# Which queue loads three of the five input tiles of a two-layer attention/FFN step

## The chip, the cores and the metric

The kernel runs on one NeuronCore of a Trainium2 chip. Five engines work side by side and meet at semaphores: TensorE (PE in the profile, its weight loads PEld), VectorE (DVE), ScalarE (ACT), GpSimd (POOL) and SyncE (SP). SyncE computes nothing; it issues transfers. ScalarE can issue transfers too, from its own queue, in between its computing instructions and in their order. The metric is the device time of one execution in microseconds (us); the median of several runs counts.

## The reference, cut to what matters

The program is one inference step of a trunk with two layers, over 512 latent tokens (`x_sample`) and 128 context tokens (`x_prompt`), all float32. What bears on this change is the very beginning of layer 0: all five tiles of 128 tokens are RMS-normalised, scaled and shifted by a modulation (adaLN), and multiplied by the q, k, v weights.

```
def rmsnorm(x, g):
    xf = x.astype(jnp.float32)
    y = xf * lax.rsqrt(jnp.mean(xf * xf, axis=-1, keepdims=True) + EPS)
    return (y * g.astype(jnp.float32)).astype(x.dtype)

def adaln(cond, w, b):
    m = jax.nn.silu(cond) @ w + b
    return jnp.split(m[..., None, :], 6, axis=-1)
...
    for l in range(DEPTH):
        sh_ap, sc_ap, g_ap, sh_fp, sc_fp, g_fp = adaln(c_ctx, ada_w[l], ada_b[l])
        sh_as, sc_as, g_as, sh_fs, sc_fs, g_fs = adaln(c, ada_w[l], ada_b[l])
        hp = rmsnorm(xp, norm_mix_pre[l]) * (1.0 + sc_ap) + sh_ap
        hs = rmsnorm(xs, norm_mix_pre[l]) * (1.0 + sc_as) + sh_as
        if l % N_MIXERS == 0:
            qp, kp, vp = na_qkv(hp, na_w_qkv[i])
            op = blocked_attention(qp, kp, vp)
            qs, ks_, vs = na_qkv(hs, na_w_qkv[i])
            os_ = neighbourhood_attention(qs, ks_, vs, cache_na_k[:, i], cache_na_v[:, i], na_rpb[i])
...
```

## The kernel before

The tokens are five tiles of 128: latent tiles 0 to 3 and the prompt as tile 4, each 128 partitions by 1024 floats (512 KB). They are loaded once into `x0_0` to `x0_4` (the profile calls all of them `x`). The latent tokens form a grid of 8 rows by 64 columns, and latent tile t takes 16 of its columns: the access pattern has 16 steps of one token (4 KB) outside and 8 steps of 64 tokens (256 KB) inside. The prompt tile is one contiguous block.

The opening (lines 505 to 668) runs so:

- `x_load(t)` issues the load of tile t on SyncE. `const_loads` follows the first one and issues four small pieces into `cc` (conditioning vectors, biases, gains) and the 128x128 identity `ident`.
- A product of `cc` and `ident` turns the conditioning into columns `ct`; ScalarE applies SiLU and writes `scol` (L525).
- `x_norm(t)`: ScalarE squares and sums the tile (`junk`, `ss`, L539), GpSimd makes `rstd` of it (L204, L206), VectorE multiplies the tile (L541).
- `x_turn(t)`: TensorE transposes the tile in two halves of four 128x128 blocks into `tr` banks of PSUM; ScalarE copies the first half to `xT` (L553) and VectorE the second (L551). Five of eight banks are held by the value projection, so the halves go round through three banks, and a half can start only when the copy three halves earlier is done.
- `mod_rows(i)` and `mod_cols(i)`, i from 0 to 3: the modulation weights `wf` (four loads of 512 KB each, from `ada_w`) against `scolp` into `row` (PE); ScalarE copies `row` to `rs` (L574); PE turns that into columns `col`; VectorE makes the gains `gcol` and shifts `hcol` (L589 to L591); then ScalarE writes `hT[0]` (L596) and VectorE updates `xT` (L597) and writes the low part `hT[1]` (L598).
- `wsplit` loads q, k, v weights into `wr`; ScalarE casts them into `wh` (L178) and VectorE or GpSimd subtracts into `wl` (L180). `v_part` multiplies `hT` by them into `vp`.
- `na_v_cache` loads a cached value tile `vc` from ScalarE's queue (L491) and copies it to `vt` (L487).

The order in which each engine takes these instructions is set by the tile framework's scheduler when the program is built; the order of PE is fixed by hand (each PE instruction is chained to the one before). Transfers of SyncE and ScalarE share eight semaphores (`DMAHW0` to `DMAHW7`) in turn, and a transfer is issued only when the one that had its semaphore before has landed.

Of the kernel before, what the change touches and what calls it, by code (L numbers as in the profile page):

```python
# [20 lines left out]
D = 1024  # L21
# [4 lines left out]
NT = T // P  # L26
# [5 lines left out]
GW = 64  # L32
# [40 lines left out]
def raw_ap(ap, offset, dims):  # L73
    return bass.AP(tensor=ap.tensor, offset=ap.offset + offset, ap=[list(d) for d in dims])
# [30 lines left out]
def hybrid_step(ctx: ExitStack, tc: tile.TileContext, A, O):  # L105
    nc = tc.nc
# [58 lines left out]
    def x_in(t):  # L165
        return A["x_sample"][0, t * P : (t + 1) * P, :] if t < 4 else A["x_prompt"][0]
# [35 lines left out]
    def rstd_of(ss, n):  # L202
        v = sm.tile([P, 1], F32, name="var")
        nc.gpsimd.tensor_scalar(v, ss, 1.0 / n, EPS, op0=ALU.mult, op1=ALU.add)  # L204
        r = sm.tile([P, 1], F32, name="rstd")
        nc.gpsimd.tensor_tensor(r, v, mhalf, op=ALU.pow)  # L206
        return r
# [298 lines left out]
    with ExitStack() as s:  # L506
        sp = s.enter_context(pool("st"))
        xts = []

        def x_load(t):  # L510
            xt = sp.tile([P, D], F32, name=f"x0_{t}")
            if t < 4:
                nc.sync.dma_start(xt, raw_ap(A["x_sample"], 16 * t * D, [[D, 16], [GW * D, 8], [1, D]]))
            else:
                nc.sync.dma_start(xt, x_in(t))
            xts.append(xt)

        x_load(0)
        const_loads()
        sel = sp.tile([P, 2], F32, name="sel")  # L520
# [14 lines left out]
        def x_norm(t):  # L535
            xt = xts[t]
            ss = sm.tile([P, 1], F32, name="ss")
            junk = sp.tile([P, D], BF16, tag="junk", name="junk0")
            nc.scalar.activation(junk, xt, AF.Square, accum_out=ss)  # L539
            r = rstd_of(ss, D)  # L540
            nc.vector.tensor_scalar(xt, xt, r, None, op0=ALU.mult)  # L541
# [14 lines left out]
        def mod_load(i):  # L556
            out = {}
            for n in range(2):
                for h in range(2):
                    out[n, h] = sp.tile([P, 4, 256], F32, tag="wf", name="wf", bufs=7)  # L560
                    nc.sync.dma_start(out[n, h], rows(A["ada_w"][0], 4 * h, 4, D - D * n + 256 * i, 256))
            return out
# [41 lines left out]
        def wv_load(i):  # L604
            wv[i] = wsplit(rows(wqkv, 4 * i, 4, 2048, 256), 4, 256)

        def x_in_norm(ts):
            for t in ts:
                if t:
                    x_load(t)  # L610
                x_norm(t)

        x_in_norm(range(NT))
        loads[0] = mod_load(0)
        wv_load(0)
        loads[1] = mod_load(1)
# [1345 lines left out]
```

## Time and profile before

| | |
|---|---|
| time, median of 3 runs | 1548.16 us (1547.85 to 1550.32) |
| profiled execution | 1550.43 us, span of its instructions 1548.6 us |
| PE busy | 1513.5 us (98%) |
| DVE, ACT, POOL busy | 1022.3 (66%), 854.0 (55%), 702.2 (45%) us |
| DMA | 243.99 MB, mean 158 GB/s |

The span is cut in the profile into stretches and instructions, each with its start in us from the span's start. "Idle before" is the time for which an engine stood before the instruction, and the name behind the arrow is what ended it.

### The profile page before, as it was taken

The numbers are of one execution on the slowest core, as the hardware profiler recorded it, in microseconds if no ns is written. First come the engines' busy times: TensorE is split into PE (matmuls) and PEld (weight loads), VectorE is DVE, ScalarE is ACT, GpSimd is POOL, SyncE is SP. The second block draws the span as 40 slices with busy tenths as digits, with TensorE's granted clock in tenths as the row PEclk, the third lists the DMA queues.
The fourth block names the chain that finished last, engine by engine and source line by source line (L and its number), as shares of the span: only waits on it lengthen the run. The fifth ranks groups of instructions, "written<-read, shape, count | busy, mean of one in ns | idle before, by whom it ended". The sixth has DMA issues, their size and how long they took to land.

```text
span 1548.6 us, 26098 instructions
## 1 busy us (share of the span) xinstructions
PE 1513.5 (98%) x9709; PEld 1343.4 (87%) x9709; DVE 1022.3 (66%) x1648; ACT 854.0 (55%) x1624; POOL 702.2 (45%) x606
## 2 busy tenths in 40 slices
PE   6999999999999999999999999999999999999998
PEld 5988998888999999978887878778899999988886
DVE  4553343659877666755757877773988887786554
ACT  5664564646655555554544447763665665564443
POOL 1554564432355455525443464532235666542433
PEclk9999999999999999999999999999999999999999
DMA  9745454253565665388574421015433335447664
GB/s 324 199 123 161 121 134 116 64 189 125 176 225 182 222 190 162 111 279 272 174 238 153 131 67 44 2 34 196 153 115 114 120 110 158 132 161 251 226 220 131
DMA packets 196666, 243.99 MB, mean 158 GB/s; under 512 B 11484, under 2 KB 153020, under 8 KB 196540
## 3 DMA queue, kind: packets, MB, share of 16 engines
q1 hardware_dynamic: 186704, 235.74, 47.8%
q10 hardware_dynamic: 9836, 6.59, 2.5%
q8 instruction: 76, 1.25, 0.3%
q14 instruction: 50, 0.41, 0.1%
HBM read 214.38 MB, written 26.34 MB: 155 GB/s over the span
## 4 chain that ended last, share of the span: by engine, by line
PE 63%; DVE 5%; ACT 2%; issue 2%; POOL 2%; DMA 1%; POOLq 0%; DVEq 0%; ACTq 0%
PE ux L117 18%; PE acc L117 17%; PE uz L117 8%; PE gp L117 5%; PE uy L117 4%; PE po L117 3%; PE y L117 2%; PE s L117 2%; PE tp L120 2%; PE ada L117 1%; DMA wr<-in_ffn_w_down 1%; DVE t L1281 1%; POOL wl L180 1%; DMA wr<-in_ffn_w_up 1%; DVE wl L180 1%
## 5 line engine op out<-in xcount | busy, mean ns | idle before, releaser
L180 POOL TENSOR_TENSOR wl<-wr,wh 128x1024 fp32r<-128x1024 f32 x70 | 173.8, 2487 | 239.8 <-ACT wh L178 228.7
L1204 POOL TENSOR_TENSOR wl<-wr,wh 128x1024 fp32r<-128x1024 f32 x76 | 183.6, 2438 | 46.9 <-ACT wh L1203 43.3
L117 PE MATMUL ux<-B,wh 128*128 128x322 f32 x832 | 200.0, 311 | 0.9 <-ACT u L1258 0.9
L1281 DVE SCALAR_TENSOR_TENSOR t<-C,cw,t 128x644 f32<-128x644 f32 x176 | 156.4, 888 | 51.3 <-ACT t L1279 50.7
L178 ACT CAST wh<-wr 128x1024 fp32r<-128x1024 f32 x140 | 145.5, 1048 | 53.8 <-DMA wr<-in_ffn_w_down 41.1
L117 PE MATMUL acc<-wh,alo 128*128 128x512 f32 x440 | 172.3, 392 | 0.3 <-DVE alo L1173 0.3
L117 PE MATMUL acc<-wl,ahi 128*128 128x512 f32 x440 | 171.9, 391 | 0.5 <-POOL wl L180 0.5
L117 PE MATMUL acc<-wh,ahi 128*128 128x512 f32 x440 | 171.9, 391 | 0.0
L117 PE MATMUL uz<-B,wh 128*128 128x322 f32 x640 | 156.2, 312 | 0.9 <-ACT v L1258 0.9
L117 PEld LDWEIGHTS ux<-B,wh 128*128 128x128 f32 x832 | 143.6, 189 | 3.3 <-issue 1.2
L1173 DVE TENSOR_TENSOR alo<-ain,ahi 128x384 fp32r<-128x384 f32 (+1 forms) x88 | 81.8, 948 | 88.9 <-ACT ahi L1171 88.6
L117 PE MATMUL ux<-B,wl 128*128 128x322 f32 x416 | 129.5, 311 | 3.0 <-DVE wl L1204 3.0
L117 PE MATMUL qk<-hT,wh 128*128 128x384 f32 (+1 forms) x512 | 122.3, 315 | 0.0
L117 PEld LDWEIGHTS uz<-B,wh 128*128 128x128 f32 x640 | 110.9, 189 | 4.4 <-ACT v L1258 1.5
L1204 POOL TENSOR_TENSOR vl<-wr,vh 128x1024 fp32r<-128x1024 f32 x38 | 96.4, 2537 | 24.6 <-ACT vh L1203 24.3
L1203 ACT CAST wh<-wr 128x1024 fp32r<-128x1024 f32 x84 | 84.8, 1049 | 40.9 <-DVE wr L1227 40.6
L1279 ACT ACTIVATE t<-C,cw 128x644 f32<-128x644 f32 x88 | 78.6, 893 | 47.8 <-DVE C L1309 40.2
L180 DVE TENSOR_TENSOR wl<-wr,wh 128x1024 fp32r<-128x1024 f32 x70 | 91.4, 1315 | 19.3 <-ACT wh L178 18.7
L117 PE MATMUL uz<-B,wl 128*128 128x322 f32 x320 | 99.6, 311 | 0.3 <-POOL wl L1204 0.3
L117 PEld LDWEIGHTS acc<-wl,ahi 128*128 128x128 f32 x440 | 82.6, 188 | 18.9 <-POOL wl L180 0.9
L117 PEld LDWEIGHTS acc<-wh,alo 128*128 128x128 f32 x440 | 82.5, 188 | 18.7 <-DVE alo L1173 1.1
L117 PEld LDWEIGHTS acc<-wh,ahi 128*128 128x128 f32 x440 | 82.6, 188 | 17.7
(259 smaller groups left out, 3858.2 us busy)
## 6 DMA issues: line engine op xcount, KB each, us to landing
wr<-in_ffn_w_up SPq DMA_DIRECT2D x88, 512.0 KB
wr<-in_ffn_w_down SPq DMA_DIRECT2D x88, 512.0 KB
wr<-in_ada_w SPq DMA_DIRECT2D x72, 512.0 KB
act<-act SPq DMA_DIRECT2D x44, 321.0 KB
wr<-in_na_w_qkv SPq DMA_DIRECT2D x24, 512.0 KB
mod<-modrow SPq DMA_DIRECT2D x20, 512.0 KB
ain<-act SPq DMA_DIRECT2D x44, 192.0 KB
wf<-in_ada_w SPq DMA_DIRECT2D x16, 512.0 KB
```

The source lines that it names most:

```text
L117: pe(nc.tensor.matmul(*a, **k))
L120: pe(nc.tensor.transpose(*a, **k))
L178: i = nc.scalar.copy(hi, raw)
L180: j = (low or nc.vector).tensor_sub(lo, raw, f32(hi))
L1173: pin(nc.vector.tensor_sub(lo[:, 0 : c1 - c0], ain[:, 0 : c1 - c0], f32(hi[:, 0 : c1 - c0])))
L1203: nc.scalar.copy(hl[0], src)
L1204: low.tensor_sub(hl[1], src, f32(hl[0]))
L1279: nc.scalar.activation(t, taps(0), AF.Identity, bias=cw[:, 3, n : n + 1], scale=cw[:, 1, n : n + 1])
L1281: nc.vector.scalar_tensor_tensor(t, taps(d), cw[:, w, n : n + 1], t, op0=ALU.mult, op1=ALU.add)
```

## The change

Latent tiles 2 and 3 and the prompt tile are issued on ScalarE's queue; tiles 0 and 1 stay with SyncE. The four later loads are written out in the order 2, 3, 4, 1 before any of the norms, where each load stood ahead of its own norm before. The list `xts` is put back in the order of the tiles, so that norms and turns go on in the order 0 to 4.

```
@@ x_load
             if t < 4:
-                nc.sync.dma_start(xt, raw_ap(A["x_sample"], 16 * t * D, [[D, 16], [GW * D, 8], [1, D]]))
+                q = nc.scalar if t >= 2 else nc.sync
+                q.dma_start(xt, raw_ap(A["x_sample"], 16 * t * D, [[D, 16], [GW * D, 8], [1, D]]))
             else:
-                nc.sync.dma_start(xt, x_in(t))
+                nc.scalar.dma_start(xt, x_in(t))
@@ the loop over tiles
-        def x_in_norm(ts):
-            for t in ts:
-                if t:
-                    x_load(t)
-                x_norm(t)
-
-        x_in_norm(range(NT))
+        for t in (2, 3, 4, 1):
+            x_load(t)
+        xts[1:] = xts[4], *xts[1:4]
+        for t in range(NT):
+            x_norm(t)
```

The scheduler orders the opening anew on SP, ACT and DVE. PE's order is the same, and so is everything behind the opening. Names such as `x_2_155` are tile 2 of the input with a buffer number.

On SyncE, from the first transfer on, this stands before:

```order
L513 DMA x_0_134<-in_x_sample 128x1x1024
L146 DMA cc<-in_c 8x128
L147 DMA cc<-in_c_ctx 8x128
L148 DMA cc<-in_ada_b 16x128
L149 DMA cc<-in_norm_mix_pre 8x128
L150 DMA ident<-in_k_ident 128x128
L513 DMA x_1_163<-in_x_sample 128x1x1024
L513 DMA x_2_173<-in_x_sample 128x1x1024 [waits DMAHW0_49]
L513 DMA x_3_183<-in_x_sample 128x1x1024 [waits DMAHW1_49]
L515 DMA x_4_193<-in_x_prompt 128x1024 [waits DMAHW2_49]
L561 DMA wf<-in_ada_w 128x4x256 [waits DMAHW3_49]
```

and this in the change, with the semaphores waited for:

```order
L514 DMA x_0_134<-in_x_sample 128x1x1024
L146 DMA cc<-in_c 8x128
L147 DMA cc<-in_c_ctx 8x128
L148 DMA cc<-in_ada_b 16x128
L149 DMA cc<-in_norm_mix_pre 8x128
L150 DMA ident<-in_k_ident 128x128
L514 DMA x_1_161<-in_x_sample 128x1x1024 [waits DMAHW0_49]
L562 DMA wf<-in_ada_w 128x4x256 [waits DMAHW2_49]
```

Three transfers are gone from SyncE, and tile 1 now waits for a semaphore before it is issued.

On ScalarE, from its first instruction to the square of tile 4, this stands before:

```order
L491 DMA vc<-in_cache_na_v 128x256
L158 ACT_TABLE_LOAD
L158 ACTIVATE cw_78<-mhalf 128x1 [waits Pool_49]
L487 COPY vt<-vc 128x256 [waits DMAHW0_49]
L539 ACTIVATE junk_156,ss<-x_0_134 128x1024 [waits DMAHW1_49]
L525 ACTIVATE scol<-ct 128x16 [waits PE_49]
L539 ACTIVATE junk_166,ss<-x_1_163 128x1024 [waits DMAHW7_49,Activation_49]
L539 ACTIVATE junk_176,ss<-x_2_173 128x1024 [waits DMAHW0_49,Activation_49]
L553 COPY xT<-tr 128x4x128 [waits PE_49] x2
L539 ACTIVATE junk_186,ss<-x_3_183 128x1024 [waits DMAHW1_49,Activation_49]
L553 COPY xT<-tr 128x4x128 [waits PE_49]
L539 ACTIVATE junk_196,ss<-x_4_193 128x1024 [waits DMAHW2_49,Activation_49,Pool_49]
```

and this in the change, from its fourth instruction on:

```order
L514 DMA x_3_157<-in_x_sample 128x1x1024
L516 DMA x_4_159<-in_x_prompt 128x1024 [waits DMAHW1_49]
L526 ACTIVATE scol<-ct 128x16 [waits PE_49]
L540 ACTIVATE junk_164,ss<-x_0_134 128x1024
L491 DMA vc<-in_cache_na_v 128x256 [waits DMAHW4_49]
L540 ACTIVATE junk_172,ss<-x_1_161 128x1024 [waits DMAHW0_49,Activation_49]
L540 ACTIVATE junk_180,ss<-x_2_155 128x1024 [waits Activation_49]
L487 COPY vt<-vc 128x256 [waits DMAHW4_49]
L540 ACTIVATE junk_188,ss<-x_3_157 128x1024 [waits DMAHW5_49,Activation_49]
L554 COPY xT<-tr 128x4x128 [waits PE_49]
L540 ACTIVATE junk_196,ss<-x_4_159 128x1024 [waits DMAHW1_49,Activation_49,Pool_49]
L554 COPY xT<-tr 128x4x128 [waits PE_49] x3
```

`scol` stands ahead of the square of tile 0 now, the load and copy of `vc` stand among the squares, and the first copy to `xT` comes behind the square of tile 3, where it came behind that of tile 2. (The first instruction of ScalarE is now the load of tile 2.) Tile 1 waits for `DMAHW0`, the semaphore of tile 2, which went first: the square of tile 2 needs no wait for its own transfer behind that of tile 1. Tile 4 waits for `DMAHW1`, that of tile 0: the square of tile 0 has no wait for a transfer any more.

On VectorE, from the multiplication of tile 3 to the first low part of `hT`, this stands before:

```order
L541 TENSOR_SCALAR x_3_183<-x_3_183,rstd 128x1024
L541 TENSOR_SCALAR x_4_193<-x_4_193,rstd 128x1024
L551 COPY xT<-tr 128x4x128 x2
L589 SCALAR_TENSOR_TENSOR gcol<-col,colb 128x4
L591 TENSOR_TENSOR hcol<-col,colb 128x4
L590 TENSOR_TENSOR gcol<-gcol,colb 128x4
L180 TENSOR_TENSOR wl<-wr,wh 128x1024
L597 TENSOR_SCALAR xT<-xT,gcol,hcol 128x512
L597 TENSOR_SCALAR xT<-xT,gcol,hcol 128x128
L597 TENSOR_SCALAR xT<-xT,gcol,hcol 128x512
L598 TENSOR_TENSOR hT_123<-xT,hT_122 128x640
```

and this in the change:

```order
L542 TENSOR_SCALAR x_4_159<-x_4_159,rstd 128x1024
L552 COPY xT<-tr 128x4x128 x3
L180 TENSOR_TENSOR wl<-wr,wh 128x1024
L590 SCALAR_TENSOR_TENSOR gcol<-col,colb 128x4
L592 TENSOR_TENSOR hcol<-col,colb 128x4
L591 TENSOR_TENSOR gcol<-gcol,colb 128x4
L598 TENSOR_SCALAR xT<-xT,gcol,hcol 128x512
L598 TENSOR_SCALAR xT<-xT,gcol,hcol 128x128
L599 TENSOR_TENSOR hT_123<-xT,hT_122 128x640
```

The subtraction into `wl` has moved from behind `gcol` to ahead of it, and the low part of `hT` comes behind two instructions on `xT`, where it came behind three. ScalarE's cast into `wh`, from which `wl` is made, has moved up in the same way, ahead of the last copy to `xT`.

## Rows read from the trace of the kernel before

**Rows 1.** The page: span, and busy time of the engines

```profile
span 1548.6 us, 26098 instructions
PE 1513.5 (98%) x9709; PEld 1343.4 (87%) x9709; DVE 1022.3 (66%) x1648; ACT 854.0 (55%) x1624; POOL 702.2 (45%) x606
```

**Rows 2.** Stretches: busy by engine (instructions), granted clock, DMA share, GB/s

```profile
19.00:22.30 3.30, 3.30 (x30) 1.86 (x32) 0.69 (x1) 0.59 (x1) 0.00 (x0) 0.52 1.09 372
...
26.70:36.00 9.30, 7.93 (x84) 6.66 (x81) 6.23 (x15) 4.63 (x9) 0.00 (x0) 1.00 1.09 383
36.00:60.00 24.00, 24.00 (x210) 22.75 (x209) 11.20 (x24) 13.27 (x23) 11.05 (x14) 1.00 0.90 228
```

**Rows 3.** Timeline of SyncE: start, duration, transfers issued

```profile
0.72 0.68 SPq L513 DMA_DIRECT2D x<-in_x_sample  x1
...
3.06 0.36 SPq L150 DMA_DIRECT2D ident<-in_k_ident  x1
3.46 2.85 SPq L513 DMA_DIRECT2D x<-in_x_sample  x3
...
7.00 4.35 SPq L561 DMA_DIRECT2D wf<-in_ada_w  x4
```

**Rows 4.** Timeline of ScalarE, the opening

```profile
0.72 0.40 ACTq L491 DMA_DIRECT2D vc<-in_cache_na_v  x1
...
3.02 0.40 ACT L487 COPY vt<-vc 128x256 f32<-128x256 f32 x1 [0.36 <-DMA vc<-in_cache_na_v]
5.78 1.06 ACT L539 ACTIVATE junk<-x 128x1024 bf16<-128x1024 f32 x1 [2.36 <-DMA x<-in_x_sample]
...
7.40 0.18 ACT L525 ACTIVATE scol<-ct 128x16 f32<-128x16 f32 x1 [0.47 <-PE ct L120]
8.36 1.06 ACT L539 ACTIVATE junk<-x 128x1024 bf16<-128x1024 f32 x1 [0.78 <-DMA x<-in_x_sample]
...
10.53 1.06 ACT L539 ACTIVATE junk<-x 128x1024 bf16<-128x1024 f32 x1 [1.01 <-DMA x<-in_x_sample]
...
11.58 0.57 ACT L553 COPY xT<-tr 128x512 f32<-128x512 f32 x1
...
15.13 1.06 ACT L539 ACTIVATE junk<-x 128x1024 bf16<-128x1024 f32 x1
```

**Rows 5.** Transfers from 7 to 12.5 us, latent tiles alone moving

```profile
DMA packets 369, 1.32 MB, mean 241 GB/s; under 512 B 46, under 2 KB 46, under 8 KB 369
```

**Rows 6.** Transfers from 13.5 to 38 us, weights

```profile
DMA packets 9457, 9.36 MB, mean 382 GB/s; under 512 B 285, under 2 KB 9456, under 8 KB 9456
```

**Rows 7.** Timeline of PE, the opening

```profile
8.70 1.97 PE L120 MATMUL tr<-ident,x 128*128 128x128 f32 x8 [1.34 <-DVE x L541]
...
17.00 1.06 PE L120 MATMUL tr<-ident,x 128*128 128x128 f32 x8 [1.54 <-DVE x L541]
18.47 1.69 PE L120 MATMUL tr<-ident,x 128*128 128x128 f32 x8 [0.41 <-DVE x L541]
20.09 2.93 PE L117 MATMUL row<-wf,scolp 128*32 128x256 f32 x32
...
24.72 2.03 PE L117 MATMUL row<-wf,scolp 128*32 128x256 f32 x32
...
28.55 0.50 PE L117 MATMUL vp<-wh,hT 128*128 128x256 f32 x2 [1.37 <-DVE hT L598]
```

**Rows 8.** Timeline of VectorE, the opening

```profile
6.96 0.17 DVE L521 TENSOR_REDUCE sel<-ident 128x2 f32<-128x8 f32 x1 [6.96 <-DMA ident<-in_k_ident]
...
17.57 0.75 DVE L541 TENSOR_SCALAR x<-x,rstd 128x1024 f32<-128x1024 f32 x1 [0.72 <-POOL rstd L206]
...
25.02 0.16 DVE L590 TENSOR_TENSOR gcol<-gcol,colb 128x4 f32<-128x4 f32 x1
25.10 1.22 DVE L180 TENSOR_TENSOR wl<-wr,wh 128x1024 fp32r<-128x1024 f32 x1
...
27.68 0.82 DVE L598 TENSOR_TENSOR hT<-xT,hT 128x640 fp32r<-128x640 f32 x1
```

## The prediction

> **What bounds the kernel now.** I read the page first: PE is busy for 1513.5 of 1548.6 us [rows 1], so the kernel is bound by TensorE, and a change outside of it can only count where TensorE stands. Next I cut the first 60 us, where the change lies, into stretches. From 36 us on PE is busy for the whole 24.00 us, and from 26.7 to 36 it stands for 9.30 - 7.93 = 1.37 us [rows 2]. The reader should take two things from that: whatever makes PE reach its value products earlier or later passes on to the end one for one, since nothing behind takes up slack; and the only slack close by is that 1.37 us, which the timeline of PE shows as one stand before 28.55, ended by VectorE's low part of `hT` [rows 7].
>
> Then I read the timelines of SyncE, ScalarE and PE up to 25 us. The opening is a chain: tiles land, ScalarE squares each (5.78, 8.36, 10.53, ..., 15.13 [rows 4]), PE turns them until 18.47 + 1.69 = 20.16 and at once does the first modulation product until 20.09 + 2.93 = 23.02 [rows 7]. The squares of tiles 0, 1 and 2 each ended a wait for a transfer [rows 4], so the landing of `x` sets the pace early; the last two squares stand behind copies of turned halves. SyncE issues fast enough: three tiles take it 2.85 us [rows 3], while between the landings of two of them lie 10.53 - 8.36 = 2.17 us [rows 4].
>
> The transfers themselves show why. While latent tiles alone move, the rate is 241 GB/s; with weights behind them it is 382 GB/s [rows 5, 6]. 512 KB at 241 GB/s are 2.18 us, just the interval of the landings. So the tiles are limited by how they move, not by who issues them. [...]
>
> **The change, step by step.** Times are of the opening, in us from the span's start.
>
> *Tiles 0 and 2 share.* Tile 0 landed at 5.78, behind `vc`, which was issued with it [rows 4]. `vc` (128 KB, 0.54 at 241 GB/s) goes away from there and tile 2 (2.18) comes beside: both land at 5.78 - 0.54 + 2.18 = 7.42. Bounds for tile 0 are 5.24 (served first) and 7.42; I take the late one, as two queues that have work alike should end alike.
>
> *The identity.* It landed at 6.96 [rows 8], 1.18 behind tile 0. It still follows tile 0 on SyncE's queue [rows 3], while ScalarE's queue has tile 3 ready. From below it lands at 6.96 - 0.54 = 6.4; from above at 7.42 + 1.18 + 2.18 = 10.8, with all of tile 3 in between. I take 9.5, nearer to the upper end, for its many small rows have to alternate with large ones. `scol` follows 7.40 - 6.96 = 0.44 later and takes 0.18 [rows 4]; it now stands ahead of the square of tile 0, which starts at 10.1 and not at 5.78.
>
> *Tile 1.* SyncE issued it at 3.46, first of three [rows 3]; now it waits for the landing of tile 2, 7.42. Behind it on SyncE stand the `wf` loads (7.00 before [rows 3]), which start some 1.1 later; that costs nothing, since their bytes went only from 13.5 on [rows 6]. From issue to landing tile 1 took 8.36 - 3.46 = 4.9, tile 0 without `vc` 5.78 - 0.72 - 0.54 = 4.5 [rows 3, 4]. So it lands between 11.9 and 12.3, and if tile 4 comes in between (512 KB at 382 GB/s, 1.37) at 13.7. I take 12.4.
>
> *ScalarE.* A square holds it for 11.58 - 10.53 = 1.05 to 1.1 [rows 4]. Tile 0 at 10.1, issue of `vc` 0.40, tile 1 at 12.4 when it lands, tile 2 at 13.5, copy to `vt` 0.40 at 14.6, tile 3 at 15.0, the first copy to `xT` 0.57 at 16.1, tile 4 at 16.7. Before it was 15.13 [rows 4]: 1.6 late, where the first square was over 4 late. The squares now follow on each other, which gives much of the loss back.
>
> *PE's turns.* The second half of tile 1 needs the bank that the first copy to `xT` frees, at 16.7. From there seven halves are left. A half cost 1.97 / 2 = 0.98 at 8.70, and 1.06 / 2 = 0.53 at 17.00 [rows 7], the two levels of the clock (from 19.0 to 22.3 the granted clock was 0.52 [rows 2], so mostly 1.2 GHz, after the stand before 17.00 [rows 7]). At 1.2 GHz throughout the turns end at 16.7 + 6.9 = 23.6. At 2.4 GHz tile 4 decides: square at 16.7, multiplied 17.57 - 15.13 = 2.44 later [rows 4, 8], turned 18.47 - 17.57 = 0.9 after that [rows 7, 8], so from 20.0 to 21.1. I take 22.3, between them, since the turns now run without the stands that they had. The product behind them takes 2.03 at the high level and took 2.93 at 20.09 [rows 7]: it ends between 23.1 and 26.5; I take 24.4, which is 1.4 later than 23.02.
>
> *What the order gives back.* The low part of `hT` for which PE stood started at 27.68, 2.50 after `gcol` was done at 25.18, with `wl` (1.22) in between [rows 8]. In the change `wl` stands ahead of `gcol`, on time that VectorE spends waiting for the product. That takes 1.2 out of the chain, and the stand of 1.37 has room for it [rows 7]. From below the gain is nothing, if the cast into `wh`, which moved up with it, waits for its weights and holds the last copy.
>
> *Sum.* +1.4 - 1.2 = +0.2, from 0.1 - 1.2 = -1.1 to 3.5 - 1.2 = +2.3, or +3.5 without the gain. `vc` has no reader in these 25 us but its copy and costs 0.4 of ScalarE twice, counted above. Behind the opening the order is the same, and the DMA queues move the same bytes. The profiled execution took 1550.43 with a span of 1548.6, some 2 above the median of 1548.16; as the sum is a difference I put it on the median: 1548.4.
>
> **Rivals.** *Tile 1 comes too late* (slower). It is issued some 4 us later than before, and tile 4, then the `wf` loads, move beside it. At the bound of 13.7 tile 4's square starts at 18.0, and if PE stays at 1.2 GHz the turns end at 24.9 and the product at 27.8, 4.8 late; less 1.2 that is +3.6, or 1551.8. It passes 0.2% (3.1 us, about what a measurement of this kernel can tell from no change) when tile 1 lands at 13.2 or later and the clock stays low until then. For it: three squares waited for transfers before [rows 4]. Against it: the clock did rise by 17.00 after turns with stands [rows 7].
>
> *Two queues move the tiles faster.* At 382 GB/s for all of `x` tile 0 and 2 land near 5.8, tile 1 near 9.5 and tile 4's square starts near 13.8; its turns end near 18.2 to 20.7, some 1 us earlier than now on the mean. With the 1.2 of the order that is -2.3, or 1545.9. For it: 241 is far below 382 [rows 5, 6], so the engines are not at their limit. Against it: the landings stand at even intervals with the next tile always queued [rows 4], so more queued work did not help.
>
> *Nothing moves*: both effects cancel and the rest hides them. That lies inside the forecast's own range.
>
> **How the numbers follow.** The forecast (-1.1 to +1.5) has 0.70, the late tile 0.18 (0.07 of it beyond +3.1), the faster tiles 0.12 (0.02 beyond -3.1). So faster by over 0.2% has 0.02, within 0.2% 0.91, slower 0.07. The predicted time is 1548.4. The range reaches from 1546.9, into the faster tiles, to 1551.0, into the late ones; the runs of before alone scatter from 1547.85 to 1550.32.
>
> **What would show it.** In the profile of the changed kernel: the square of tile 0 starts near 10, with `scol` just ahead; that of tile 1 ends a wait for its transfer near 12.4; tile 4's is near 16.7; the first modulation product ends near 24.4; the stand of PE on the low part of `hT` is nearly gone; and from 36 us on PE is dense as before, with the same instructions within 1 us. The rate from 3 to 12 us stays near 241 GB/s. The prediction is wrong if the first product ends before 23 (faster transfers, or an early clock), or after 27 (late tile 1 or low clock), or if a difference arises behind 60 us, where I count none.

## The result and the profile after

The changed kernel takes 1552.53 us (median of 20 runs, 1549.92 to 1553.73), the kernel before 1548.44 us (20 runs, 1546.32 to 1550.49). The ratio is 1.0024, 95% interval 1.0018 to 1.0031: slower by 3.7 us (2.8 to 4.8; the medians differ by 4.1). Forecast were 1548.4 us and a range up to 1551.0.

The page of the changed kernel (span; busy time by engine), against [rows 1]:

```profile
span 1550.8 us, 26095 instructions
...
PE 1511.2 (97%) x9709; PEld 1343.2 (87%) x9709; DVE 1023.2 (66%) x1648; ACT 853.6 (55%) x1624; POOL 700.7 (45%) x606
```

PE does the same work and stands longer. The stretches, against [rows 2] (columns as there):

```profile
19.00:22.30 3.30, 2.57 (x22) 2.10 (x21) 3.06 (x5) 2.61 (x6) 0.89 (x3) 1.00 1.09 385
26.70:36.00 9.30, 8.54 (x82) 7.15 (x74) 6.79 (x16) 5.05 (x9) 0.00 (x0) 0.82 1.05 367
31.70:35.10 3.40, 3.40 (x19) 3.40 (x18) 2.77 (x6) 2.01 (x4) 0.00 (x0) 0.54 1.09 382
36.00:60.00 24.00, 24.00 (x223) 22.04 (x214) 11.21 (x24) 13.82 (x24) 9.16 (x14) 1.00 0.89 238
```

A stretch at the lower level of the clock (1.2 GHz) lay at 19.0 to 22.3 before, on the last turns and the first modulation product (2.93 long). Here it lies at 31.7 to 35.1 (granted 0.54), on dense value products. SyncE, against [rows 3]:

```profile
5.42 0.57 SPq L514 DMA_DIRECT2D x<-in_x_sample  x1
9.04 2.06 SPq L562 DMA_DIRECT2D wf<-in_ada_w  x4
```

Tile 1 is issued at 5.42, when tile 2 has landed. ScalarE, against [rows 4]:

```profile
7.69 0.36 ACTq L516 DMA_DIRECT2D x<-in_x_prompt  x1
11.42 0.18 ACT L526 ACTIVATE scol<-ct 128x16 f32<-128x16 f32 x1 [8.49 <-PE ct L120]
11.43 0.34 ACTq L491 DMA_DIRECT2D vc<-in_cache_na_v  x1
11.51 1.05 ACT L540 ACTIVATE junk<-x 128x1024 bf16<-128x1024 f32 x1
...
12.68 1.06 ACT L540 ACTIVATE junk<-x 128x1024 bf16<-128x1024 f32 x1
...
16.35 0.41 ACT L487 COPY vt<-vc 128x256 f32<-128x256 f32 x1 [1.35 <-DMA vc<-in_cache_na_v]
...
17.72 0.56 ACT L554 COPY xT<-tr 128x512 f32<-128x512 f32 x1
18.18 1.06 ACT L540 ACTIVATE junk<-x 128x1024 bf16<-128x1024 f32 x1
```

Tile 0 landed at 7.69 (the prompt tile waits for it), its square starts at 11.51, behind `scol`. The square of tile 1 comes at 12.68, with no wait shown. Between the squares of tiles 2 and 3 ScalarE stands 1.35 for the cached value tile, which was issued only at 11.43, behind `scol`, and the first copy to `xT` comes at 17.72, where it was at 11.58 [rows 4]. VectorE, against [rows 8]:

```profile
10.98 0.17 DVE L522 TENSOR_REDUCE sel<-ident 128x2 f32<-128x8 f32 x1 [10.98 <-DMA ident<-in_k_ident]
...
23.42 1.21 DVE L180 TENSOR_TENSOR wl<-wr,wh 128x1024 fp32r<-128x1024 f32 x1
...
27.74 0.80 DVE L598 TENSOR_SCALAR xT<-xT,gcol,hcol 128x512 f32<-128x512 f32 x2 [0.94 <-ACT hT L597]
```

PE, against [rows 7]:

```profile
18.33 1.09 PE L120 MATMUL tr<-ident,x 128*128 128x128 f32 x8 [1.10 <-ACT xT L554]
19.86 1.53 PE L120 MATMUL tr<-ident,x 128*128 128x128 f32 x12 [0.43 <-ACT xT L554]
21.68 1.09 PE L120 MATMUL tr<-ident,x 128*128 128x128 f32 x8 [0.30 <-DVE xT L552]
22.70 1.93 PE L117 MATMUL row<-wf,scolp 128*32 128x256 f32 x32
...
29.45 0.51 PE L117 MATMUL vp<-wh,hT 128*128 128x256 f32 x2 [0.76 <-DVE hT L599]
...
41.87 1.93 PE L117 MATMUL row<-wf,scolp 128*32 128x256 f32 x32
```

The turns stand for the copies to `xT`. The first modulation product ends at 22.70 + 1.93 = 24.63, 1.61 later than 23.02 [rows 7]. The last row is the fourth modulation product, behind the stretch in which everything differs. The timeline of PE in the kernel before has it here:

```profile
39.45 1.93 PE L117 MATMUL row<-wf,scolp 128*32 128x256 f32 x32
```

So the change is 2.42 us late there in this execution: +1.61 at the first product, -0.73 for the order (the rest of the sum), +1.54 for the low clock (the way from first to fourth product takes 41.87 - 22.70 = 19.17, and 40.77 - 23.14 = 17.63 in the third execution of the change, which has no low stretch, below).

### The profile page after: what moved, and what is told of

Same layout as the page of the kernel before. It is cut to its first block, busy times and chain, and to the rows that moved or that the text cites. A ratio compares the mean times of both kernels' runs of the same rounds, so it can differ in the third digit from the quotient of the medians.

```text
span 1550.8 us, 26095 instructions
## 1 busy us (share of the span) xinstructions
PE 1511.2 (97%) x9709; PEld 1343.2 (87%) x9709; DVE 1023.2 (66%) x1648; ACT 853.6 (55%) x1624; POOL 700.7 (45%) x606
## 4 chain that ended last, share of the span: by engine, by line
PE 63%; DVE 6%; ACT 2%; issue 2%; DMA 2%; POOL 1%; ACTq 0%; POOLq 0%; DVEq 0%
PE acc L117 18%; PE ux L117 18%; PE uz L117 8%; PE uy L117 4%; PE gp L117 4%; PE po L117 3%; PE y L117 2%; PE s L117 2%; PE tp L120 2%; PE ada L117 1%; DVE t L1280 1%; DMA wr<-in_ffn_w_up 1%; DMA gn<-in_gqa_k_norm 1%; DVE wl L180 1%; DVE xo L400 0%
## 5 line engine op out<-in xcount | busy, mean ns | idle before, releaser
L117 PEld LDWEIGHTS acc<-wh,ahi 128*128 128x128 f32 x440 | 82.5, 188 | 17.7
```

The source lines that it names most:

```text
L117: pe(nc.tensor.matmul(*a, **k))
```

## The experiments

The start of the fourth product is used below as the measure of the opening; before it is 39.45 and 39.52 in two executions, 39.49 on the mean.

**The change and the kernel before, unchanged.** Both were run again, and the change in three more single executions. In what follows, "change 1" is the execution shown above, "change 2" that of the repeat, and "change 3" to "change 5" are the single ones; the other kernels with more than one execution are numbered in the same way.

> The changed kernel once more, nothing edited, to see what of its profile comes back. Theory A (the opening): the identity lands near 11 again, the first modulation product ends near 24.6, and PE is 1 to 2.5 us late at 40 us; the ratio to the kernel before is 1.001 to 1.003. Theory B (the loss lies behind 100 us, in waits that fall differently in each execution): PE's lateness at 100 us is under 1 us and what is added behind it sits at other places than at 851, 922 and 1443 us.

> The kernel before once more, nothing edited, as the scale for every other run: ratio 1.000 within 0.001. Its profile against the first one of the kernel before: theory A expects the opening equal within 0.3 us up to 100 us and shifts of up to 1 us behind it; theory B expects shifts behind 100 us as large as those between the kernel before and the changed one (up to 2 us).

> The changed kernel, one look more. Both its profiles so far had a stretch of 3.4 us at a granted clock of 0.5 at 31.7 us; of its timed executions most had a mean clock that has no room for such a stretch behind the first rise, and were as slow. Theory C: in those the clock rises for the first time only at 25 us or later, so that the last turns and the first product run at 1.2 GHz, and PE is as late (2 to 3 us) at 40 us. Rival: the clock rises by 22 us, no low stretch follows, PE is about 1 us late at 40 us, and the rest arises behind 60 us.

> The same kernel and question as the look before: where the clock rises first, and how late PE is at 40 us and at 1500 us.

> The same kernel and question as the two looks before: where the clock rises first, and how late PE is at 40 us and at 1500 us.

Measured: the change 1.0026 (1.0017 to 1.0035), the kernel before 1.0001 (0.9992 to 1.0009); changes 3 to 5 took 1549.82, 1552.98 and 1553.0 us. The low stretch of the clock is not the cause alone: it shows in changes 1 and 2, and those of 1552.98 and 1553.0 have none. Nor does the clock rise only behind the first product in them: it is 1.93 long in all five. What changes 4 and 5 have instead is in the timelines of change 4, first SyncE, then ScalarE, then PE:

```profile
7.80 0.56 SPq L514 DMA_DIRECT2D x<-in_x_sample  x1
```

```profile
13.93 1.06 ACT L540 ACTIVATE junk<-x 128x1024 bf16<-128x1024 f32 x1 [1.85 <-DMA x<-in_x_sample]
...
16.65 0.41 ACT L487 COPY vt<-vc 128x256 f32<-128x256 f32 x1 [0.40 <-DMA vc<-in_cache_na_v]
```

```profile
16.84 1.11 PE L120 MATMUL tr<-ident,x 128*128 128x128 f32 x4 [1.03 <-DVE x L542]
18.63 5.63 PE L120 MATMUL tr<-ident,x 128*128 128x128 f32 x28 [0.68 <-ACT xT L554]
24.19 1.93 PE L117 MATMUL row<-wf,scolp 128*32 128x256 f32 x32
```

Tile 2 lands at 7.80, not at 5.42, so tile 1 is issued 2.4 later; its square waits 1.85 for it, and PE stands 1.03 before its turn. The copy to `vt` still ends a wait for `vc` (0.40), and PE stands again, 0.68 for the first copy to `xT` behind it. After these stands the remaining 28 transposes take 5.63, 0.20 each, between the 0.25 of the lower level (1.97 for 8) and the 0.13 of the upper (1.06 for 8) [rows 7].

**The constants first.**

```
-        x_load(0)
         const_loads()
+        x_load(0)
```

> The changed kernel with the four constants and the identity issued ahead of tile 0 on SyncE: the identity should land before 5 and not at 11, the square of tile 0 start when that tile lands, near 8. Theory A: the opening gets about 3 us earlier than in the changed kernel, the first product ends near 22, and the time falls to that of the kernel before or below it (ratio 0.999 to 1.000). Rival (three more instructions on ScalarE and three fewer on SyncE shift something behind the opening): the ratio stays at 1.002, since the counts are those of the changed kernel.

Measured: 1.0019 (1.0010 to 1.0028). The identity landed by 8.34 instead of 10.98, but tile 0 only at 10.49, and the first product started at 23.57. The late identity alone is not the loss. Nor is tile 1: its square started at 12.67, as in change 1. What stood in the way is on ScalarE and on PE:

```profile
16.49 0.41 ACT L487 COPY vt<-vc 128x256 f32<-128x256 f32 x1 [1.49 <-DMA vc<-in_cache_na_v]
17.85 0.56 ACT L554 COPY xT<-tr 128x512 f32<-128x512 f32 x1
```

```profile
18.47 5.15 PE L120 MATMUL tr<-ident,x 128*128 128x128 f32 x28 [1.78 <-ACT xT L554]
```

`vc` was issued 0.9 earlier than in change 1 (10.50) and still landed only at 16.5; PE stood 1.78 for the first copy to `xT` behind it.

**One queue, constants last** (the kernel before, with all five tiles issued from SyncE ahead of the constants).

```
-        x_load(0)
+        for t in range(NT):
+            x_load(t)
         const_loads()
```

> The kernel before, one queue, with all five tiles issued ahead of the constants and the identity. No transfer changes its queue, but the identity lands behind all tiles, near 15, and all turns wait for it. Theory A: the first product ends 2 us or more behind the 23.0 of the kernel before, near 25, and the time is slower by about that, ratio 1.001 to 1.003, though no second queue is in use. Rival (the second queue itself costs the time): ratio 1.000.

Measured: 1.0013 (1.0003 to 1.0023). The squares came no later than before (5.88 to 13.91), and the turns waited for the identity, then ran in one go (timeline of PE):

```profile
14.86 0.30 PE L120 MATMUL ct<-ident,cc 40*128 40x40 f32 x1 [14.86 <-DMA ident<-in_k_ident]
15.09 6.52 PE L120 MATMUL tr<-ident,x 128*128 128x128 f32 x40
21.54 1.94 PE L117 MATMUL row<-wf,scolp 128*32 128x256 f32 x32
```

Turns that begin 6.4 us later than in the kernel before (15.09 against 8.70 [rows 7]) end only 1.45 later (21.61 against 20.16), since nothing stands between them; the forecast of its expectation, a first product that ends near 25, missed by 1.5 (23.48). The fourth product started at 39.17, 0.3 earlier than before; behind it PE stood 0.86 for the low part of `hT` at 49.44, where the kernel before has no stand, so that here the fourth product isn't the last word. An identity that comes at 14.86 cost no more than the change, where its reader started at 10.98.

**The prompt tile alone on ScalarE's queue** (the kernel before).

```
-                nc.sync.dma_start(xt, x_in(t))
+                nc.scalar.dma_start(xt, x_in(t))
```

> One part of the change alone: only the prompt tile is issued on ScalarE's queue, as its first transfer; the four latent tiles stay on SyncE in their order, and the orders of the engines stay nearly those of the kernel before (vc's load comes behind the table load). Theory (what lies ahead on the second queue lands first and takes its time from the tile and the constants that are needed first): tile 0 and the identity land 1 to 1.5 us later (near 7.2 and 8.5), tiles 2 and 3 land as before, the squares from tile 2 on are where they were, and the ratio is 1.000 within 0.0008. Rival (any transfer on the second queue delays the first product): the product ends 1 us or more later than 23.0 and the ratio is 1.001 or more.

Measured: 1.0007 (0.9998 to 1.0016), not to be told from no change; the fourth product started at 39.66. The tile that is moved last does no harm that shows.

**Dummy transposes against the clock.** Transposes of the identity into columns of a `vp` bank that nothing reads fill PE's stands among the turns: 21 in the change, 15 in the kernel before (at the halves (1,0), (3,0), (4,0)).

```
+                for _ in range({(0, 0): 12, (1, 1): 6, (2, 0): 1, (3, 1): 1, (4, 0): 1}.get((t, q), 0)):
+                    turn(vb[0][:, 256:384], ident, ident)
```

> The changed kernel with 21 more transposes of the identity into unused columns of a PSUM bank, placed where PE stood during the turns (12 ahead of tile 0, 6 ahead of the second half of tile 1, one at three more places); every other engine keeps its order. Theory (about 1.5 us of the loss is the stretch at a granted clock of 0.5 at 31.6 to 35 us, which fell on dense work since the turns had run with stands): with PE busy earlier the low stretch goes away or falls on the turns, PE's lateness at 40 us falls from 2.4 to 2.8 to about 1.3, and the ratio to near 1.0015. Rival (the low stretch falls where it likes): it stays, and the ratio stays at 1.0025 or more.

> The kernel before with 15 more transposes of the identity in the stands of PE between the turns (2 ahead of tile 1, 10 ahead of tile 3, 3 ahead of tile 4); all other orders as before. There the low clock lay at 19.0 to 22.4, on the last turns and the first product (2.93 us and not 1.93). Theory: the level stays high there, the first product ends about 1 to 1.5 us earlier, and the time falls by up to that (ratio 0.9993). Rival (the low stretch is only put off to the dense work behind): the first product is earlier, but PE's lead is gone by 40 us, ratio 1.000 or above.

Measured: 1.0015 (1.0006 to 1.0024) and 1.0011 (1.0002 to 1.0020). In the change the fourth product then started at 41.12, against 41.80 on the mean of five executions of the change, but changes 1 to 5 reach from 40.77 to 42.25 by themselves, and the intervals of the two ratios overlap, so that a share of the clock in the loss is likely and not shown by this run. Tile 1 was issued at 8.35 here, and `vt` waited for `vc` as in the change. In the kernel before it went the other way (timeline of PE, then the stretch):

```profile
19.70 1.93 PE L117 MATMUL row<-wf,scolp 128*32 128x256 f32 x32
...
23.33 1.07 PE L117 MATMUL row<-wf,scolp 128*32 128x256 f32 x16
26.14 0.64 PE L117 MATMUL row<-wf,scolp 128*32 128x256 f32 x8 [1.74 <-DMA wf<-in_ada_w]
27.43 0.99 PE L117 MATMUL row<-wf,scolp 128*32 128x256 f32 x8 [0.65 <-DMA wf<-in_ada_w]
```

```profile
26.70:36.00 9.30, 8.65 (x58) 7.59 (x57) 5.00 (x12) 2.88 (x5) 0.00 (x0) 0.63 1.09 385
```

The first product came 0.4 earlier and the second had to wait 1.74 + 0.65 for its weights; then the clock fell (0.63 of the stretch), and the fourth product started at 42.24, 2.8 late. A first product that comes earlier gained nothing in this execution.

**The first product three more times** (the kernel before; the extra products go to a bank that nothing reads).

```
+        idle = bk.get("row")
+        for _ in range(3):
...
+        bk.put(idle)
```

> The kernel before with the first modulation product done three times more on PE ahead of the real one, into a bank that nothing reads: 3 x 1.93 = 5.8 us of PE work on the path, and nothing else added. The scheduler moves the cast into wh and the subtraction into wl ahead of the gains, as in the changed kernel, which gives back 0.7. Theory (lateness of the opening reaches the end one for one): PE is 5 us late at 40 us and at 1500 us, ratio near 1.0033. Rival (slack behind the opening takes up a part): the lateness shrinks from 40 to 100 us by more than 1 us, and the ratio is below 1.0025.

Measured: 1.0075 (1.0062 to 1.0088), +11.6 us; the four products are 7.11 long where the one was 2.93. The stretch behind it:

```profile
34.70:41.70 7.00, 6.91 (x33) 6.91 (x34) 4.32 (x12) 2.29 (x4) 0.00 (x0) 0.52 0.79 276
```

The fourth product started at 48.68, 9.2 late: the first product started 0.8 later already, 4.2 were added, and behind them PE's stand on `hT` grew from 1.37 [rows 7] to 2.66 and the stretch at 0.52 followed. So the forecast ratio of 1.0033 missed, and the run is no clean measure of one for one; but nothing behind took any of the 9.2 up.

**The cached value tile loaded first**, as in the kernel before.

```
+        vts_of[0] = na_v_tile()
+        na_v_cache(vts_of[0], 0)
         x_load(0)
         const_loads()
```

> The changed kernel with one transfer put back: the cached value tile vc is again the first on ScalarE's queue, ahead of tile 2. In the changed kernel its copy to vt stood 1.35 and 0.52 us for vc, and that copy holds up the square of tile 3. Theory (the wait for vc is a part of the loss): the copy waits no more, tile 4's square starts some 1 to 1.5 us earlier (near 17 and not 18.2), the first product ends near 23.5 to 24, ratio near 1.0015 to 1.002 and not 1.0025. Rival (the tiles' landing or the identity set the pace alone): the first product ends where it did, 24.6 to 25.0, and the ratio stays near 1.0025.

> The change with the load of the cached value tile first on ScalarE's queue, one look. If its ratio of 1.0000 hangs on the timing of instructions (theory S or T), the turns run in one go from about 15.9 us, the first product ends near 24.4 us and PE is within 1 us of the kernel before at 40 us, again. If it hung on where the granted clock happened to fall, a low stretch of the clock or a rise later than 23 us may show here, with 1.5 us or more of lateness at 40 us.

> As the look before it; two looks of one kernel show how far the granted clock's rise and its low stretch move from one execution to the next.

> The kernel of r2_vc_first again, unchanged. It was 1.0000 [0.9991, 1.0009] with PE 0.1 to 0.7 us late at 40 us in three executions and up to 1.7 us late at 1440 us. Expected 1.0000 to 1.0009; above 1.0012 the earlier ratio was a lucky one and loading the value tile first gives back only a half of the loss.

Measured: 1.0000 (0.9991 to 1.0009) and 1.0006 (0.9998 to 1.0015), value first 2 and 3 took 1550.19 and 1549.84 us. Most of the loss is gone with this one edit. It does three things. The copy to `vt` is done by 3.5 and waits for nothing later; the first copy to `xT` comes ahead of the square of tile 3 again; and, as the value tile takes the first semaphore of the eight, tile 1 now waits for the semaphore of tile 0 (`DMAHW1`), not for that of tile 2. Timelines of SyncE and PE in value first 4:

```profile
5.74 0.57 SPq L514 DMA_DIRECT2D x<-in_x_sample  x1
```

```profile
14.15 4.57 PE L120 MATMUL tr<-ident,x 128*128 128x128 f32 x24 [3.02 <-DVE x L544]
19.26 1.06 PE L120 MATMUL tr<-ident,x 128*128 128x128 f32 x8 [0.54 <-DVE x L544]
20.73 1.06 PE L120 MATMUL tr<-ident,x 128*128 128x128 f32 x8 [0.41 <-DVE x L544]
21.73 1.93 PE L117 MATMUL row<-wf,scolp 128*32 128x256 f32 x32
```

No turn stands for a copy to `xT` any more, and 24 transposes of the first turns run without a stand.

**Only the copy to `vt` moved** behind the turns; its load, all semaphores of the tiles and the order of SyncE stay as in the change.

```
-        na_v_cache(vts_of[0], 0)
         vb = [bk.get("vp") for _ in range(NT)]
...
         mod_cols(1, rs)
+        na_v_cache(vts_of[0], 0)
```

> The change, with the copy of the cached value tile into `vt` written behind the turns; its load stays where the change has it, behind the prompt tile on ScalarE's queue. On ScalarE the copy then stands behind the third copy to `xT`, and the first copy to `xT` comes ahead of the square of tile 3, as before the change. Theory S (the wait of that copy on ScalarE, and the copy to `xT` behind it, make the loss): the turns run with hardly a stand from about 16 us, the first product ends 0.6 to 1.0 us later than before, ratio 1.0000 to 1.0012. Rival T (the late transfers make the loss: identity at 10.2 to 11.1 us in the change, 9.9 where the value tile is loaded first): the identity lands at 10.2 to 11.1 again and the loss stays, ratio 1.0018 to 1.0031 as for the change.

> The kernel of r4_value_copy_late again, unchanged, now beside the value tile loaded first. There it was 0.73 us late at 40 us but 1.0015 [1.0006, 1.0024] in time. By theory S (copy and its wait) PE is again 0.5 to 1.0 us late at 40 us, with no turns at the low level behind 18 us, and the ratio lies at 1.0000 to 1.0012, the same as that of r5_value_load_first_again within its interval. By rival T (late transfers) it is 1.0015 to 1.0031 and above that of r5_value_load_first_again by 0.001 or more.

Measured: 1.0015 (1.0006 to 1.0024) and 1.0017 (1.0008 to 1.0026). Theory S (the copy and its wait alone) falls: the loss went down by about a third only. T, as it was put, does not hold either: the identity's reader started at 11.16 and 10.54 here, and at 10.72 to 11.04 in value first 2 to 4. What differs between the two executions of this very kernel is tile 1 (SyncE and PE of the first, then of the second):

```profile
5.68 0.57 SPq L514 DMA_DIRECT2D x<-in_x_sample  x1
```

```profile
14.59 6.41 PE L120 MATMUL tr<-ident,x 128*128 128x128 f32 x32 [3.02 <-DVE x L542]
21.57 1.06 PE L120 MATMUL tr<-ident,x 128*128 128x128 f32 x8 [0.57 <-DVE x L542]
22.56 1.93 PE L117 MATMUL row<-wf,scolp 128*32 128x256 f32 x32
```

```profile
7.98 0.57 SPq L514 DMA_DIRECT2D x<-in_x_sample  x1
```

```profile
13.97 1.97 PE L120 MATMUL tr<-ident,x 128*128 128x128 f32 x8 [3.02 <-DVE x L542]
17.26 6.61 PE L120 MATMUL tr<-ident,x 128*128 128x128 f32 x32 [1.31 <-DVE x L542]
23.79 1.93 PE L117 MATMUL row<-wf,scolp 128*32 128x256 f32 x32
```

Tile 1 issued 2.3 later leaves PE standing 1.31 before its turn, and the first product starts 1.23 later. With the copy to `vt` out of the way, a tile 1 on time brings the fourth product to 40.24, near the kernels with the value tile first; a late one leaves it at 41.48.

**Value tile and constants first.** This is the edit of the value tile in the kernel with the constants first.

```
+        const_loads()
+        vts_of[0] = na_v_tile()
+        na_v_cache(vts_of[0], 0)
         x_load(0)
-        const_loads()
```

> The change with the value tile first on ScalarE's queue and the constants first on SyncE's. Tile 0 then lands near 10 us instead of 7, the identity near 8; `vt` has no wait among the squares, but the second copy to `xT` comes behind the square of tile 4. If late copies to `xT` make the loss, the turns stand once more and the ratio is 1.0008 to 1.0020; if only the wait for the value tile does, 0.9995 to 1.0008.

Measured: 1.0007 (0.9998 to 1.0016), the fourth product at 39.77, though one turn stood 0.38 for a copy to `xT` and the first squares came no earlier (10.73, 13.18). It cannot be told from the value tile first alone. Against the constants first alone the fourth product is 1.4 earlier (39.77, 41.19), although the square of tile 1 is 0.5 later (13.18, 12.67). No version of the change came out faster than the kernel before.

**Executions side by side** (us from the span's start, from the timelines):

| kernel | tile 1 issued | its square | copy to `vt` | 1st copy to `xT` | 1st product | 4th product | span |
|---|---|---|---|---|---|---|---|
| before 1 | 3.46 | 8.36 | 3.02 | 11.58 | 20.09 | 39.45 | 1548.6 |
| before 2 | 3.46 | 8.41 | 2.95 | 11.66 | 20.17 | 39.52 | 1546.7 |
| change 1 | 5.42 | 12.68 | 16.35 | 17.72 | 22.70 | 41.87 | 1550.8 |
| change 2 | 7.38 | 13.62 | 16.47 | 17.83 | 23.08 | 42.25 | 1549.9 |
| change 3 | 8.01 | 14.21 | 16.78 | 18.14 | 23.14 | 40.77 | 1548.0 |
| change 4 | 7.80 | 13.93 | 16.65 | 18.02 | 24.19 | 41.86 | 1551.2 |
| change 5 | 8.22 | 14.87 | 17.50 | 18.86 | 24.62 | 42.24 | 1551.2 |
| constants first | 5.63 | 12.67 | 16.49 | 17.85 | 23.57 | 41.19 | 1548.5 |
| copy late 1 | 5.68 | 13.01 | 21.08 | 15.74 | 22.56 | 40.24 | 1547.7 |
| copy late 2 | 7.98 | 14.35 | 22.37 | 16.58 | 23.79 | 41.48 | 1548.8 |
| value first 1 | 5.86 | 13.01 | 3.10 | 15.25 | 22.45 | 40.09 | 1546.9 |
| value first 2 | 5.81 | 13.44 | 2.99 | 15.67 | 22.54 | 40.18 | 1548.4 |
| value first 3 | 6.00 | 12.98 | 2.91 | 15.62 | 21.98 | 39.62 | 1548.0 |
| value first 4 | 5.74 | 12.79 | 3.01 | 15.31 | 21.73 | 39.37 | 1549.1 |

In changes 1 to 5 and with the constants first, the copy to `vt` ended a wait for `vc` every time (1.35, 0.52, 0.24, 0.40, 0.31 and 1.49), and behind it PE stood for the first copy to `xT` (0.53 to 1.78). Where tile 1 waits for tile 2 (change, copy late), it is issued at 5.4 to 5.7 in two executions and at 7.4 to 8.2 in five; where it waits for tile 0 (value first), at 5.7 to 6.0 in all four.

## Why the prediction was wrong

**The step that failed** is ScalarE's chain up to the first copy to `xT`: "copy to `vt` 0.40 at 14.6, tile 3 at 15.0, the first copy to `xT` 0.57 at 16.1". That PE's last seven halves hang on this copy was right. But it started at 17.7 to 18.9 in the five executions of the change, and PE went on at 18.3 to 19.5 and not at 16.7. Two terms ahead of it were wrong.

*The wait for `vc`* was put at nothing: "`vc` has no reader in these 25 us but its copy and costs 0.4 of ScalarE twice, counted above". Its load now stands behind `scol`, and so behind the identity. Issued at 10.5 to 11.5, it landed 4.9 to 6.0 later, with other loads moving beside it; as the first transfer of the kernel before it took 2.3 (from 0.72 to 3.02 [rows 4]). So the copy to `vt` started at 16.35 to 17.50 and not at 14.6, and it ended a wait for `vc` in all five.

*Tile 1*: "it lands between 11.9 and 12.3, and if tile 4 comes in between ... at 13.7. I take 12.4". This held in change 1 (its square at 12.68 shows no wait) and failed in the four others. I let tiles 0 and 2 end together at 7.42 and tile 1 take 4.5 to 4.9 from there. In fact one of the two comes first, tile 2 lands at 7.4 to 8.2 in these four, and tile 1 then takes 6.1 to 6.7 (13.93 - 7.80 = 6.13; 14.87 - 8.22 = 6.65). Its square starts at 13.6 to 14.9. That is the rival "tile 1 comes too late", which had a chance of 0.18 and was the usual case. It put the first product too late, as PE was at the upper clock when that started (1.93 long in every execution): the product ended 1.6 to 3.5 late, not 4.8. The measured time is above that rival's 1551.8 all the same.

The two waits overlap, so taking away one leaves the other. With tile 1 on time and `vc` late, the first copy to `xT` is as late as ever (17.72 in change 1, 17.85 with the constants first). With the copy to `vt` out of the way and tile 1 late, PE stands 1.31 for tile 1, and the fourth product is 2.0 late (copy late 2). Where both are out of the way it starts at 39.4 to 40.2.

That the first product ended at 24.63 in change 1, beside the 24.4 of the forecast, is luck: PE went on 1.6 later than forecast, and needed 4.37 for the turns that were left where 22.3 - 16.7 = 5.6 were forecast.

**Point by point.** *Rate and sharing*: the Trainium skill, "DMA: Bandwidth & Descriptors", says under "Issuing engines are not separate DMA queues" that a second issuing engine saves issue time alone, and the trace agrees: 7 to 12.5 us moved at 243 GB/s, against 241 [rows 5] (transfers of change 1; in changes 2 to 5, where the prompt tile was issued 1.5 to 2.1 earlier, it was 257 to 279):

```profile
DMA packets 561, 1.34 MB, mean 243 GB/s; under 512 B 88, under 2 KB 256, under 8 KB 561
```

*Identity*: taken at 9.5 with an upper bound of 10.8; its reader started at 10.98, outside. The first square came at 11.5 instead of 10.1; with the value tile first its reader is as late (9.87 to 11.04) and the loss is gone, and with the constants first it is early and the loss stays. *Tile 4*: its square started at 18.2 (forecast 16.7). *Turns and first product*: forecast end 24.4, bounds 23.1 to 26.5; measured 24.63 to 26.55. *Order of `wl`*: it stands ahead of `gcol` as forecast, but gave 0.7, not 1.2: the stand on `hT` fell from 1.37 [rows 7] to 0.76, while VectorE's update of `xT` now waits 0.94 for ScalarE, which reads the same `xT` for `hT`; that this wait takes the rest was not tried. *Clock*: I counted it in the turns alone. In changes 1 and 2 a stretch of 3.4 us at the lower level fell on dense products from 31.7 on and cost 1.54.

*Sum*: the opening is late by 2.3 on the mean of five executions (41.80 - 39.49), from 1.3 to 2.8, where +0.2 was forecast. The first product's end makes +2.4 of it (forecast +1.4), the order -0.7 (forecast -1.2), and the low stretch, 1.54 in two of five, +0.6 (not in the forecast). *Nothing behind takes up slack* is not contradicted: from the fourth product to the end of the span it takes 1507.2 to 1509.3 in the change and 1507.2 and 1509.2 in the kernel before.

**What stays open.** The medians differ by 4.1, the openings by 2.3. The stretch behind scatters by 2.1 us from one execution to the next in either kernel, so seven executions can't place the rest; that the change adds something there is neither shown nor excluded. Loading the value tile first brings back nearly all of the time, not only the 2.3, but it changes three things together: the wait for `vc`, the place of the first copy to `xT`, and the tile for which tile 1 waits. Moving the copy alone gave back about a third of the loss. How the rest splits between `vc` and tile 1 is not settled; a kernel in which only tile 1's semaphore differs was not tried.

## What to carry to other kernels

Before loads are spread over two queues, write down which earlier transfer each load's semaphore belongs to: two transfers that started together did not end together here, and a load that waits for the later one can pay the difference. Look also at what slides in between on the issuing engine: a small load with a copy, harmless as the first instruction, held ScalarE for up to 1.35 us in the middle of a chain, since it was issued late and landed later still. Where two waits overlap, an experiment that takes away one of them shows less than its share. This chain, bound by the rate of its transfers, gained nothing from a second queue, and its order got worse.

## What was not expected of the hardware

Of two 512 KB transfers issued within 0.01 us on two queues, now one and now the other landed first, 1.2 to 2.3 us ahead: tile 2 at 5.42 and tile 0 at 7.69 in change 1, tile 0 at 5.64 and tile 2 at 7.80 in change 4 (times at which the loads that waited for them were issued). With tile 2 issued 0.5 later (1.21), behind the value tile, tile 1, which waits for tile 0 there, was issued at 5.7 to 6.0 in all four executions. The low stretch of the clock, 3.4 us at 0.54, came some 9 us after the first product had run at the upper level, in two of five executions; PE was busy in all of it, and had stood 0.70 before 25.34 and 0.76 before 29.45 in change 1. Change 3 had the same stands and no such stretch. Where the upper level begins moves as well: 28 transposes behind a stand took 4.45 in change 3 and 5.63 in change 4. The Trainium skill, "TensorE: Matmul & The Clock Gate", says in its part on the clock gate that the number of matmuls at the lower rate differs between runs of one kernel; these executions agree.
